# Two blocks of the expert product U moved beside the query projections, in buffers of their own

## The chip, the cores and the metric

The kernel runs on one core of a Trainium2 chip. The metric is the device time of one execution in microseconds (us), and lower is better. Engine names follow the profile: PE is TensorE (PEld its weight loads), DVE VectorE, ACT ScalarE, POOL GpSimd, SP SyncE; SPq and POOLq are their DMA queues.

## What is computed

The program is one decoder layer on 512 tokens of width 1024 in float32. Sparse attention, forgetting attention and their output projection come first. The part that matters here is the second half, PEER retrieval over 128 x 128 = 16384 single-neuron experts, with 8 heads of 16 experts each:

```python
q = (hc @ w_q).reshape(-1, PEER_HEADS, PEER_KEY_DIM)
s1 = einsum('chd,nd->chn', q[..., :half], k1); s2 = einsum('chd,nd->chn', q[..., half:], k2)
v1, i1 = top_k(s1, 16); v2, i2 = top_k(s2, 16)
best_s, best_pos = top_k(v1[..., :, None] + v2[..., None, :], 16)   # over the 256 sums
g = softmax(best_s)
act = gelu(einsum('cd,chkd->chk', hc, u[expert]))
out = einsum('chk,chkd->cd', g * act, v[expert])
```

## The kernel before, in words

**How PEER is computed.** The tokens stand in four tiles of 128. For tiles 0 to 2 nothing is gathered: U is multiplied with all 384 tokens, 128 blocks of 128 experts (`u_block`), each result goes through Gelu to a tile `a`, a dense matrix of gate weights (`gates`, p_g, stored in the DRAM tiles `g_d`) says how much each token wants of each expert, and V is multiplied with gates times `a` (`v_load`, `v_mm`, output acc). For tile 3 the chosen rows of U and V are gathered by indirect DMA (gu, gv) beside the V stage.

**Products in three parts.** `mm3` (L149 to L151) multiplies in three passes: each operand is split into a rounded part hi and a rest lo. So a block of U loads `raw` on SP's queue (L879), writes hi on ScalarE (L882), lo on VectorE (L887) or, for the odd blocks from 5 to 51, by ScalarE and an accumulating DMA on POOL's queue (L884, L885), and then has 8 x 3 = 24 matmuls of 384 columns (p_u). Gelu of the result is L893. The first 22 blocks store their `a` in DRAM (`a_d`, L895), since only 34 fit on the chip; the V stage reads those back as `ar` (L1004). The second operand is `h2`, the normed tokens of tiles 0 to 2; tile 3 has its own `h2l`.

**The stages around the change.** `residual` and `peer_norm` finish tile 3 (xn at L642, transposes at L647, hf at L650, h2l at L651 and L652). Then two halves of the query projection follow (p_q, `wchunks` of `w_pq` on L135 to L143), their transposes (tp_q, L863), and per tile and half a `route`: scores p_sc (L722, a bank of tag "tp") and sixteen best per side on VectorE (MAX8, MATCH_REPLACE8 and FIND_INDEX8, L729 to L733). Behind the projections their pool `wo` (in the stack `wst`) is closed and the pool `up` is opened on its memory (L869 to L871). `u_ahead(n)` (L901) makes the next n blocks, up to NAHEAD = 56: 4, then 2, then 2 in each of the 24 rounds of gates, then what is left. After that PSUM is handed over and the V stage begins, in which the other 72 blocks of U run between the blocks of V.

**What sets the order.** The framework orders the instructions of each engine when the program is built, by priority (the place in the program) and its own estimate of when each is ready; engines then run in that order. The load and the splits of a block carry a priority 1000 instructions ahead of their place (`tc.high_priority(offset=UPRI)`, L877); its matmuls have the priority of their place. Pools are stacked on two sides of SBUF; a tile in memory that a closed pool held waits, tile by tile, for the last user of what it overlaps. In `up` the blocks have three raw, two hi and three lo buffers and two for a stored `a`. Their PSUM banks go round the tags "pj", "po" and "ix", one bank each: "pj" also holds tp_q, "po" the attention's output, "ix" the transposes of `peer_norm`.

Of the kernel before, what the change touches and what calls it, by code (L numbers as in the profile page):

```python
# [9 lines left out]
F32 = mybir.dt.float32  # L10
F32R = mybir.dt.float32r
# [10 lines left out]
P = 128  # L22
D = 1024
KC = D // P
# [14 lines left out]
DT = ND * P  # L39
NACT = 34  # L40
# [15 lines left out]
PACE = 1.02  # L56
UPOOL = ()
LAST = 4
URB = 3
UDMA = tuple(range(5, 53, 2))  # L60
VRB = 3
# [15 lines left out]
def hybrid_layer(ctx: ExitStack, tc, x, pos, wada, wada_n, cols, w_small, w_in_a, w_in_b, wuk, wuv,  # L77
# [3 lines left out]
    def opened(stack, name, **kw):  # L81
        if "space" not in kw:
            kw["reuse_waits"] = "tile"
        return stack.enter_context(tc.tile_pool(name=name, bufs=1, **kw))
# [8 lines left out]
    def one(name, tag="tp"):  # L93
        return ps.tile([P, 512], F32, tag=tag, name=name, bufs=BANKS[tag])
# [53 lines left out]
    def mm3(o, ahi, alo, bhi, blo, start, stop, **kw):  # L148
        nc.tensor.matmul(o, ahi, bhi, start=start, stop=False, **kw)  # L149
        nc.tensor.matmul(o, ahi, blo, start=False, stop=False, **kw)  # L150
        nc.tensor.matmul(o, alo, bhi, start=False, stop=stop, **kw)  # L151
# [24 lines left out]
    def row_back(s, pl, tag, bufs):  # L176
        t = pl.tile([P, D], F32, tag=tag, name=f"gate{s}", bufs=bufs)
        nc.sync.dma_start(t, row_d[s].to_broadcast([P, D]))
        return t
# [95 lines left out]
    for half in range(2):  # L275
# [3 lines left out]
        for k in range(KC):  # L279
            a, b = eff[0][:, k:k + 1], mods[0][:, k:k + 1]  # L280
# [337 lines left out]
    wst = ExitStack()  # L618
# [86 lines left out]
    rt = ExitStack()  # L705
# [147 lines left out]
    for n in range(2):  # L853
# [12 lines left out]
                route(n, j - RLAG, *lists[j - RLAG])  # L866
        for j in range(NT - RLAG if n == 0 else NT, NT):
            route(n, j, *lists[j])
    wst.close()  # L869
    rq = opened(rt, "rq")  # L870
    up = opened(ctx, "up", side="right")  # L871


    acts = []

    def u_block(b, psum):
        with tc.high_priority(offset=UPRI):  # L877
            raw = up.tile([P, KC, P], F32, tag="raw", name=f"u{b}", bufs=URB)
            nc.sync.dma_start(raw.rearrange("p k e -> p (k e)"), ut[b])  # L879
            hi = up.tile([P, KC, P], F32R, tag="hi", name=f"uhi{b}", bufs=2)  # L880
            lo = up.tile([P, KC, P], F32R, tag="lo", name=f"ulo{b}", bufs=3)
            nc.scalar.activation(hi, raw, AF.Copy)  # L882
            if b in UDMA:
                nc.scalar.activation(lo, raw, AF.Copy, scale=-1.0)  # L884
                nc.gpsimd.dma_start(lo.rearrange("p k e -> p (k e)"), raw.rearrange("p k e -> p (k e)"), accum_op=ALU.add)  # L885
            else:
                (nc.gpsimd if b in UPOOL else nc.vector).tensor_tensor(lo, raw, hi.bitcast(F32), op=ALU.subtract)  # L887
        o = psum(f"p_u{b}")[:, :DT]
        for k in range(KC):
            mm3(o, hi[:, k], lo[:, k], h2[0][:, k], h2[1][:, k], k == 0, k == KC - 1)  # L890
        spilt = b < NSPILL
        a = up.tile([P, DT], F32, tag="as" if spilt else "a", name=f"a{b}", bufs=2 if spilt else NACT)
        nc.scalar.activation(a, o, AF.Gelu)  # L893
        if spilt:
            nc.sync.dma_start(a_d[b], a)  # L895
            a = a_d[b]
        acts.append(a)

    nu = [0]

    def u_ahead(n):  # L901
        for _ in range(n):
            if nu[0] < NAHEAD:
                u_block(nu[0], lambda n: one(n, ("pj", "po", "ix")[nu[0] % 3]))
                nu[0] += 1

    def chosen(j):
        sel3 = choose(j, *lists[j])
        if j == NT - 1:
            nc.vector.scalar_tensor_tensor(e0, sel3[:, 0], float(NK), sel3[:, 1], op0=ALU.mult, op1=ALU.add)  # L910
            nc.vector.tensor_copy(g0, sel3[:, 2])
        return sel3
# [30 lines left out]

    route(1, 0, *lists[0])
    u_ahead(U0[0])
    sel3 = chosen(0)
    u_ahead(U0[1])
    waiting = []

# [4 lines left out]
    for j, coming in ((0, (3, 1)), (1, (2,)), (2, ())):  # L954
        tt = spread(j, sel3)
        for tg in range(P // 16):
            for half in range(2):
                waiting.append((j, tg, half, hot(j, tg, half, *tt)))
            gates_all()
            for i, jn in enumerate(coming):  # L960
                if tg == WHEN[i][0]:
                    route(1, jn, *lists[jn])
                if tg == WHEN[i][1]:
                    sel3 = chosen(jn)
            u_ahead(GPAT[tg])
            for _ in range(NGP[tg] if j == ND - 1 else 0):
                next(gen)
# [14 lines left out]
    def v_load(b):  # L982
        if b % 8 == 0:
            gt = vp.tile([P, ND, P // 16, 8, 16], F32, tag="gt", name=f"gt{b}", bufs=2)
            for j in range(ND):
                nc.sync.dma_start(gt[:, j].rearrange("p g i t -> p g (i t)"),
                                  g_d[j][:, :, b:b + 8, :].rearrange("p g i t -> p g (i t)"))
            gts[0] = gt
        raw = vp.tile([P, D], F32, tag="raw", name=f"v{b}", bufs=VRB)
        nc.sync.dma_start(raw, pv[b * P:(b + 1) * P, :])  # L990
        late = b >= NK - LAST + VB
        if late:
            hi = up.tile([P, D], F32R, tag="hi", name=f"vhi{b}", bufs=2)
            lo = up.tile([P, D], F32R, tag="lo", name=f"vlo{b}", bufs=3)
        else:
            hi = vp.tile([P, D], F32R, tag="vhi", name=f"vhi{b}", bufs=VB)
            lo = vp.tile([P, D], F32R, tag="vlo", name=f"vlo{b}", bufs=VB)
        nc.scalar.activation(hi, raw, AF.Copy)  # L998
        nc.vector.tensor_tensor(lo, raw, hi.bitcast(F32), op=ALU.subtract)  # L999
        w = vp.tile([P, DT], F32, tag="w", name=f"w{b}", bufs=2)  # L1000
        a = acts[b]
        if b < NSPILL:
            a = vp.tile([P, DT], F32, tag="ar", name=f"ar{b}", bufs=ARB)
            nc.sync.dma_start(a, acts[b])  # L1004
        nc.vector.tensor_tensor(w.rearrange("p (g t) -> p g t", t=16), a.rearrange("p (g t) -> p g t", t=16),
                                gts[0][:, :, :, b % 8, :].rearrange("p j g t -> p (j g) t"), op=ALU.mult)
        if late:
            wh, wl = (up.tile([P, DT], F32R, tag="a", name=f"{n_}{b}", bufs=NACT) for n_ in ("wh", "wl"))
        else:
            wh = vp.tile([P, DT], F32R, tag="wh", name=f"wh{b}", bufs=VB)  # L1010
            wl = vp.tile([P, DT], F32R, tag="wl", name=f"wl{b}", bufs=VB)
        nc.scalar.activation(wh, w, AF.Copy)  # L1012
        last[0] = nc.vector.tensor_tensor(wl, w, wh.bitcast(F32), op=ALU.subtract).ins  # L1013
        return wh, wl, hi, lo
# [29 lines left out]

    steps = [RATE[0 if b < NSPILL else 1 if b < NK - NACT else 2] for b in range(NK - LAST)]
    due = 0.0
    tail = []
    for b in range(NK):
        ops = v_load(b)
        if b < NK - LAST:  # L1050
            for j in range(ND):
                v_mm(b, j, *ops)
        else:
            tail.append((b, ops))
        if b >= NSPILL and nu[0] < NK:
            u_block(nu[0], two)
            nu[0] += 1
        if b == NK - 24:
            gf = up.tile([P, D], F32, tag="raw", name="gf", bufs=URB)
            nc.sync.dma_start(gf, gfin.to_broadcast([P, D]))  # L1060
            gate2 = row_back(5, up, "raw", URB)
        if b < len(steps):
            due += steps[b] * (2 * TOPK - sum(NGP)) * PACE / sum(steps)
            while due >= 1.0:
                next(gen, None)
                due -= 1.0
# [69 lines left out]
```

## Time and profile before

| what | us |
|---|---|
| median of three runs | 1609.1 |
| lowest and highest run | 1595.54 and 1612.48 |
| the profiled execution | 1605.42 |
| its span in the trace | 1603.6 |

The span runs from the first to the last instruction of the trace. Times in the rows below are us from its start. A timeline row gives start, duration, engine, line, operation, output and inputs, the count, and in brackets the idle time ahead of it with what ended it.

### The profile page before, as it was taken

The numbers are of one execution on the slowest core, as the hardware profiler recorded it, in microseconds if no ns is written. First come the engines' busy times: TensorE is split into PE (matmuls) and PEld (weight loads), VectorE is DVE, ScalarE is ACT, GpSimd is POOL, SyncE is SP. The second block draws the span as 40 slices with busy tenths as digits, with TensorE's granted clock in tenths as the row PEclk, the third lists the DMA queues.
The fourth block names the chain that finished last, engine by engine and source line by source line (L and its number), as shares of the span: only waits on it lengthen the run. The fifth ranks groups of instructions, "written<-read, shape, count | busy, mean of one in ns | idle before, by whom it ended". The sixth has DMA issues, their size and how long they took to land.

```text
span 1603.6 us, 23086 instructions
## 1 busy us (share of the span) xinstructions
PE 1504.2 (94%) x8136; PEld 1321.3 (82%) x8138; DVE 1257.6 (78%) x2649; ACT 732.1 (46%) x1166; POOL 518.4 (32%) x413
## 2 busy tenths in 40 slices
PE   6888798998899999899999999999999999999996
PEld 6657587776699889789788999999999999998885
DVE  6698986856999999743567898888887888786886
ACT  4655446454156678665333333333333333333333
POOL 2323113112000220200013565554555555553420
PEclk7999899999999999999999999999999999999998
DMA  8233233522168987978877999999998999997974
GB/s 341 80 118 106 98 135 109 162 75 83 50 175 240 274 267 241 307 223 255 304 261 262 345 392 355 326 353 321 345 350 322 353 323 347 345 315 252 336 246 149
DMA packets 158277, 398.35 MB, mean 248 GB/s; under 512 B 12480, under 2 KB 68688, under 8 KB 154832
## 3 DMA queue, kind: packets, MB, share of 16 engines
q1 hardware_dynamic: 116832, 248.81, 46.2%
q0 software_dynamic: 40320, 146.82, 26.1%
q8 instruction: 64, 1.05, 0.3%
q10 hardware_dynamic: 1008, 1.24, 0.2%
q14 instruction: 53, 0.43, 0.1%
HBM read 350.54 MB, written 33.69 MB: 240 GB/s over the span
## 4 chain that ended last, share of the span: by engine, by line
PE 67%; DVE 12%; DMA 8%; ACT 6%; issue 5%; POOL 1%; SPq 0%; DVEq 0%; POOLq 0%; ACTq 0%
PE acc L1020 28%; PE p_u L151 9%; PE p_u L150 9%; PE p_u L149 9%; DMA ulo<-u 3%; PE po L562 2%; PE p_g L843 2%; ACT st L846 1%; PE p_b L149 1%; PE tp L552 1%; PE p_b L151 1%; PE p_b L150 1%; PE pl L536 1%; DMA wa<-in_wada_dram 1%; DVE ulo L887 1%
## 5 line engine op out<-in xcount | busy, mean ns | idle before, releaser
L151 PE MATMUL p_u<-h,ulo 128*128 128x384 f32 x1024 | 349.6, 341 | 10.2 <-DMA ulo<-u 10.1
L149 PE MATMUL p_u<-h,uhi 128*128 128x384 f32 x1024 | 348.9, 341 | 1.3 <-ACT a L893 1.3
L150 PE MATMUL p_u<-h,uhi 128*128 128x384 f32 x1024 | 347.1, 339 | 0.0
L919 POOL DMA_INDIRECT gu<-in_un_dram,e x128 | 191.3, 1495 | 275.4 <-DVE gu L927 238.6
L882 ACT ACTIVATE uhi<-u 128x1024 fp32r<-128x1024 f32 x128 | 135.9, 1062 | 283.5 <-PE p_u L150 277.7
L919 POOL DMA_INDIRECT gv<-in_pv_dram,e x128 | 195.5, 1527 | 180.4 <-DVE acc L938 153.2
L1020 PE MATMUL acc<-vhi,wh 128*128 128x512 f32 x768 | 237.3, 390 | 2.6 <-ACT wh L1012 2.6
L1020 PE MATMUL acc<-vlo,wh 128*128 128x512 f32 x768 | 237.4, 389 | 0.8 <-DVE vlo L999 0.8
L1020 PE MATMUL acc<-vhi,wl 128*128 128x512 f32 x768 | 237.0, 389 | 0.0
L1012 ACT ACTIVATE wh<-w 128x384 fp32r<-128x384 f32 x128 | 67.3, 526 | 316.3 <-issue 187.9
L151 PEld LDWEIGHTS p_u<-h,ulo 128*128 128x128 f32 x1024 | 194.5, 190 | 13.7 <-DMA ulo<-u 13.1
L149 PEld LDWEIGHTS p_u<-h,uhi 128*128 128x128 f32 x1024 | 194.6, 190 | 4.7 <-ACT a L893 1.7
L150 PEld LDWEIGHTS p_u<-h,uhi 128*128 128x128 f32 x1024 | 194.4, 190 | 3.6 <-issue 0.7
L1013 DVE TENSOR_TENSOR wl<-w,wh 128x384 fp32r<-128x384 f32 x128 | 71.3, 557 | 135.3 <-ACT wh L1012 135.1
L1020 PEld LDWEIGHTS acc<-vlo,wh 128*128 128x128 f32 x768 | 144.0, 188 | 31.3 <-DVE vlo L999 1.4
L1020 PEld LDWEIGHTS acc<-vhi,wl 128*128 128x128 f32 x768 | 144.2, 188 | 30.0
L938 DVE SCALAR_TENSOR_TENSOR acc<-gv,w,acc 128x1024 f32<-128x1024 f32 x127 | 162.4, 1279 | 5.6 <-DMA gv<-in_pv_dram,e 5.4
L1020 PEld LDWEIGHTS acc<-vhi,wh 128*128 128x128 f32 x768 | 143.2, 188 | 27.7 <-ACT wh L1012 3.3
L927 DVE SCALAR_TENSOR_TENSOR gu<-gu,h2n 128x1024 f32<-128x1024 f32 x128 | 154.0, 1220 | 15.4 <-DMA gu<-in_un_dram,e 15.4
L887 DVE TENSOR_TENSOR ulo<-u,uhi 128x1024 fp32r<-128x1024 f32 x104 | 126.9, 1220 | 49.3 <-ACT uhi L882 49.2
L999 DVE TENSOR_TENSOR vlo<-v,vhi 128x1024 fp32r<-128x1024 f32 x128 | 156.1, 1219 | 4.1 <-ACT vhi L998 3.8
L998 ACT ACTIVATE vhi<-v 128x1024 fp32r<-128x1024 f32 x128 | 135.5, 1059 | 10.2 <-PE acc L1020 4.3
(355 smaller groups left out, 2348.3 us busy)
## 6 DMA issues: line engine op xcount, KB each, us to landing
u<-in_ut_dram SPq DMA_DIRECT2D x128, 512.0 KB, 5.8
v<-in_pv_dram SPq DMA_DIRECT2D x128, 512.0 KB, 5.2
g_d<-st SPq DMA_DIRECT2D x24, 1024.0 KB, 6.2
gt<-g_d SPq DMA_DIRECT2D x48, 512.0 KB, 9.5
wada<-in_wada_dram SPq DMA_DIRECT2D x32, 512.0 KB, 3.3
ulo<-u POOLq DMA_DIRECT2D x24, 512.0 KB, 8.2
raw_b<-in_w_in_b_dram SPq DMA_DIRECT2D x12, 512.0 KB, 3.7
a_d<-a SPq DMA_DIRECT2D x22, 192.0 KB, 4.1
```

Of the source, the lines that this page charges most:

```text
L149: nc.tensor.matmul(o, ahi, bhi, start=start, stop=False, **kw)
L150: nc.tensor.matmul(o, ahi, blo, start=False, stop=False, **kw)
L151: nc.tensor.matmul(o, alo, bhi, start=False, stop=stop, **kw)
L882: nc.scalar.activation(hi, raw, AF.Copy)
L887: (nc.gpsimd if b in UPOOL else nc.vector).tensor_tensor(lo, raw, hi.bitcast(F32), op=ALU.subtract)
L919: nc.gpsimd.indirect_dma_start(out=t, out_offset=None, in_=src, in_offset=bass.IndirectOffsetOnAxis(ap=e0[:, s:s + 1], axis=0))
L927: nc.vector.scalar_tensor_tensor(t, t, 1.0, h2n, op0=ALU.mult, op1=ALU.mult, accum_out=dot0[:, s:s + 1])
L938: nc.vector.scalar_tensor_tensor(acc0, t, w0[:, s:s + 1], acc0, op0=ALU.mult, op1=ALU.add)
L998: nc.scalar.activation(hi, raw, AF.Copy)
L999: nc.vector.tensor_tensor(lo, raw, hi.bitcast(F32), op=ALU.subtract)
L1013: last[0] = nc.vector.tensor_tensor(wl, w, wh.bitcast(F32), op=ALU.subtract).ins
L1020: nc.tensor.matmul(accs[2 * j + n], l[:, js], r[:, n * 512:(n + 1) * 512], start=b == 0 and i == 0, stop=b == NK - 1 and i == 2)
```

## The change

Blocks 0 and 1 of U (`UEARLY = 2`) are issued at the end of the query projections, before the pool of the query weights is closed, from a pool `ue` of their own, opened under the same stack. It has one raw buffer, two hi, two lo and one stored `a`. The later blocks use `up` as before. The three PSUM tags are turned by one place, so that block 0 takes "po", block 1 "ix" and block 2 "pj". The calls of `u_ahead` behind it are as before.

```diff
+UEARLY = 2
...
-    wst.close()
-    rq = opened(rt, "rq")
-    up = opened(ctx, "up", side="right")
...
     def u_block(b, psum):
         with tc.high_priority(offset=UPRI):
-            raw = up.tile([P, KC, P], F32, tag="raw", name=f"u{b}", bufs=URB)
+            raw = up.tile([P, KC, P], F32, tag="raw", name=f"u{b}", bufs=URB if b >= UEARLY else 1)
             nc.sync.dma_start(raw.rearrange("p k e -> p (k e)"), ut[b])
             hi = up.tile([P, KC, P], F32R, tag="hi", name=f"uhi{b}", bufs=2)
-            lo = up.tile([P, KC, P], F32R, tag="lo", name=f"ulo{b}", bufs=3)
+            lo = up.tile([P, KC, P], F32R, tag="lo", name=f"ulo{b}", bufs=3 if b >= UEARLY else 2)
...
-        a = up.tile([P, DT], F32, tag="as" if spilt else "a", name=f"a{b}", bufs=2 if spilt else NACT)
+        a = up.tile([P, DT], F32, tag="as" if spilt else "a", name=f"a{b}", bufs=(2 if b >= UEARLY else 1) if spilt else NACT)
...
     def u_ahead(n):
         for _ in range(n):
             if nu[0] < NAHEAD:
-                u_block(nu[0], lambda n: one(n, ("pj", "po", "ix")[nu[0] % 3]))
+                u_block(nu[0], lambda n: one(n, ("po", "ix", "pj")[nu[0] % 3]))
                 nu[0] += 1
+
+
+    up = opened(wst, "ue", side="right")
+    u_ahead(UEARLY)
+    wst.close()
+    rq = opened(rt, "rq")
+    up = opened(ctx, "up", side="right")
```

## Rows read from the trace of the kernel before

**Rows 1.** The page: busy us, share of the span and instructions of each engine.
```profile
PE 1504.2 (94%) x8136; PEld 1321.3 (82%) x8138; DVE 1257.6 (78%) x2649; ACT 732.1 (46%) x1166; POOL 518.4 (32%) x413
```
**Rows 2.** The page: the chain that ended last, by engine and line.
```profile
PE acc L1020 28%; PE p_u L151 9%; PE p_u L150 9%; PE p_u L149 9%; DMA ulo<-u 3%; PE po L562 2%; PE p_g L843 2%; ACT st L846 1%; PE p_b L149 1%; PE tp L552 1%; PE p_b L151 1%; PE p_b L150 1%; PE pl L536 1%; DMA wa<-in_wada_dram 1%; DVE ulo L887 1%
```
**Rows 3.** Busy time by stretch; the last columns: granted clock, DMA share, GB/s.
```profile
375.30:379.00 3.70, 0.45 (x3) 0.21 (x2) 2.42 (x4) 1.90 (x4) 2.21 (x7) 0.97 0.88 302
...
428.20:435.20 7.00, 2.20 (x8) 1.60 (x8) 7.00 (x53) 3.19 (x4) 0.00 (x0) 0.87 0.43 150
435.20:440.20 5.00, 5.00 (x16) 4.55 (x15) 5.00 (x22) 0.00 (x0) 0.00 (x0) 0.50 0.44 136
...
430.00:768.00 338.00, 308.67 (x2175) 291.40 (x2175) 263.94 (x886) 222.86 (x271) 42.16 (x47) 0.97 0.81 248
```
**Rows 4.** Timeline of PE at the query projections.
```profile
359.74 0.60 PE L583 MATMUL tp_m<-cst_t,ob 128*128 128x128 f32 x4
...
378.79 1.12 PE L647 MATMUL tp_g<-cst_t,xn 128*128 128x128 f32 x4 [3.25 <-DVE xn L642]
...
429.07 0.66 PE L863 MATMUL tp_q<-cst_t,qn 128*128 128x128 f32 x4 [0.75 <-ACT qn L860]
433.77 2.08 PE L722 MATMUL p_sc<-keys_t,qT 128*128 128x256 f32 x4 [4.05 <-DVE iu L732]
```
**Rows 5.** Instructions on the raw tiles of U: duration ns min/median/max, first and last start.
```profile
L882 ACT ACTIVATE uhi<-u x128: 1042/1062/1121, 430.3 to 1435.8; 128x1024 fp32r<-128x1024 f32 x128
L887 DVE TENSOR_TENSOR ulo<-u,uhi x104: 1199/1220/1228, 435.1 to 1436.9; 128x1024 fp32r<-128x1024 f32 x104
...
DMA to landing us min/median/max: 3.4/6.4/14.9
```
**Rows 6.** Timeline of SP's queue at the first loads of U.
```profile
379.40 65.34 SPq L879 DMA_DIRECT2D u<-in_ut_dram  x6
```
**Rows 7.** Timeline of ACT at the first Gelu.
```profile
443.14 1.28 ACT L893 ACT_TABLE_LOAD   x1
444.44 0.49 ACT L893 ACTIVATE a<-p_u 128x384 f32<-128x384 f32 x1
```
**Rows 8.** Timeline of DVE from the last norm to the first routing.
```profile
384.76 0.70 DVE L651 CAST h2l<-hf 128x1024 fp32r<-128x1024 f32 x1 [5.42 <-ACT hf L650]
...
389.06 0.48 DVE L729 MAX8 v<-p_sc 128x8 f32<-128x128 f32 x2
```
**Rows 9.** Timeline of PE from the last gates to the first V block.
```profile
744.66 0.62 PE L843 MATMUL p_g<-oh,oh 128*128 128x128 f16 x8 [0.57 <-ACT st L846]
...
750.03 0.33 PE L149 MATMUL p_u<-h,uhi 128*128 128x384 f32 x1
...
754.19 0.33 PE L149 MATMUL p_u<-h,uhi 128*128 128x384 f32 x1
...
768.23 0.73 PE L1020 MATMUL acc<-vhi,wh 128*128 128x512 f32 x2 [1.68 <-ACT wh L1012]
```
**Rows 10.** Timeline of SP's queue from the last store of gates on.
```profile
747.27 0.33 SPq L849 DMA_DIRECT2D g_d<-st  x1
751.36 0.33 SPq L879 DMA_DIRECT2D u<-in_ut_dram  x1
...
755.52 0.34 SPq L879 DMA_DIRECT2D u<-in_ut_dram  x1
755.96 0.52 SPq L986 DMA_DIRECT2D gt<-g_d  x1
...
760.06 0.43 SPq L1004 DMA_DIRECT2D ar<-a_d  x1
```
**Rows 11.** DMA issues from 720 to 800: KB each, median us to landing.
```profile
gt<-g_d SPq DMA_DIRECT2D x9, 512.0 KB, 7.2
g_d<-st SPq DMA_DIRECT2D x3, 1024.0 KB, 6.2
```
**Rows 12.** Timeline of ACT ahead of the first V block.
```profile
767.65 0.52 ACT L1012 ACTIVATE wh<-w 128x384 fp32r<-128x384 f32 x1 [1.76 <-DVE w L1005]
```

## Prediction, made before the changed kernel was run

> **What bounds the kernel now.** The profiled execution took 1605.4 us for a span of 1603.6, so 1.8 us lie outside the span. The median of the three runs is 1609.1 (1595.5 to 1612.5). I sum against 1605.4 and add the 3.7 us between the two at the end. The page's busy line comes first: TensorE is at 94%, VectorE at 78% and the others below half [rows 1]. The chain that ended last agrees: most of it is TensorE, in p_u and in acc [rows 2]. So work taken off TensorE counts only if TensorE is busy where it is taken away, and work put on it is free only where TensorE is idle.
>
> The stage table shows such idle places at the query projections. In 375.3 to 379 TensorE is busy 0.45 us of 3.7; in 428.2 to 435.2 it is busy 2.2 of 7.0; and in 435.2 to 440.2, where block 0 of U starts, the granted clock is 0.50, the 1.2 GHz level, after that idle time [rows 3]. The instructions name the causes. The first hole is 3.25 us before the transposes of the last tile's norm, waiting for VectorE's xn. The second is 4.05 us before p_sc, waiting for VectorE's index search (L732): the top-16 routing has filled VectorE by then [rows 4]. From 430 to 768 TensorE is busy 308.7 us of 338 [rows 3], so there it is the limit, with some 9% of stalls.
>
> **Part 1: two blocks leave the late stage.** A block is 24 matmuls. Two of them that are 24 matmuls apart start at 750.03 and 754.19, so a block takes 4.16 us, 0.173 us a matmul [rows 9], and two take 8.3. The number of blocks made ahead stays 56, and the calls behind the change ask for 4, 2, 24 times 2, and then for what is left. Before, 2 are left for the very end; now none are. So two blocks go from behind the last gates to before the first: -8.3 us of TensorE work after 768 at the most.
>
> **Part 2: the same two run earlier.** The new pool lies just below the query weights, on memory of the attention stage. Its raw tile falls on the last attention outputs, which the transposes of L583 read at 359.74 [rows 4]; the hi and lo tiles fall on older ones. So u0 can be loaded from about 360.4. From block times in the trace (load to landing 6.4 us, hi 1.06, lo 1.22 [rows 5]) block 0 is split by about 369, and block 1, which shares the single raw buffer, by about 379. h2 of the three tiles they multiply is long there. Block 0 can use bank "po" at once. Block 1 needs "ix", which the last norm gives back near 384. Their matmuls were issued behind the projections in the program, so they fill holes: 3.25 us at 375.5, and 4.05 us at 429.7 with 0.75 us of waiting ahead of it. That is 8.05 us of cover for 8.3 us of work: +0.3. If they are put between projections instead, the projections end later, but p_sc then waits so much less for VectorE, and the sum is the same. Without any cover the cost would be 8.3.
>
> The other instructions of the moved steps: two loads of 512 KB and two stores of 192 KB on SP. SP issued six loads of u from 379.40 over 65 us [rows 6], so it was waiting for memory and not for its turn; the moved ones stand ahead of these and delay nothing, unless u0 is queued before 360 and holds up the projection weights (a rival below). On ScalarE hi and Gelu, 1.06 and 0.49 us per block [rows 5, 7], find an engine that is busy 1.9 of 3.7 and 3.2 of 7.0 us in the two holes [rows 3]. On VectorE two lo of 1.22 us fit in the 5.42 us of idle time before h2l [rows 8]; if they fall behind 389, where VectorE is full, they cost 2.4. That is also what VectorE saves later; I count nothing for it (bounds 0 and -2.4), because from 430 on TensorE is the fuller of the two, 308.7 us against 263.9 [rows 3].
>
> **Part 3: the clock.** In 435.2 to 440.2 there are 16 matmuls in 5.0 us, which take 16 x 0.173 = 2.8 at 2.4 GHz. If blocks 0 or 1 run in the hole before, block 2 starts at full clock: -2.2 us. The bounds are 0, when the hole stays, and -2.2.
>
> **Part 4: what waits next at the other end.** The gain of part 1 has to pass the start of the V stage. The last p_g starts at 744.66 and is done at 745.28; the first acc starts at 768.23, 22.95 us behind it. In between lie nearly five blocks of p_u, to 766.5, and then 1.68 us of idle time [rows 9]. After the change nearly three blocks are left, 12.5 us. But the V stage also needs the gates: the store g_d is issued at 747.27 [rows 10], 2.0 us behind the last p_g, lands 6.2 us later, and gt, read back from it, needs 7.2 us [rows 11]; then wh, 0.52 [rows 12], behind w, which is a product of the same size and taken as long. That makes 2.0 + 6.2 + 7.2 + 1.1 = 16.5 us, if nothing else holds SP. SP's queue shows that something does: prefetches of u are issued at 751.36 and 755.52, each when a raw buffer comes free, and only behind them gt's third part at 755.96 and ar at 760.06 [rows 10]. These loads (u56 to u58 before, u58 to u60 after) are paced by the blocks behind the last gates, so they can stand in the same place: 22.95 us, no gain at all. Bounds 16.5 and 22.95, and I take the middle, 19.7, since neither end is nearer to a row: -3.2 us instead of -8.3.
>
> TensorE is then idle from 12.5 to 19.7 us, longer than the 4.05 us that left it at 0.50 before. The V stage starts cold: +2.2 by the same 5 us stretch (bounds 0, for V loads that are late anyway, and 2.5).
>
> The moment of the last p_g itself moves little: 52 blocks stand ahead of the last gates in the program before (0 to 51), and behind 435 just as many after (2 to 53). It gains part 3's 2.2 and loses part 2's 0.3.
>
> **Sum.** -2.2 + 0.3 - 3.2 + 2.2 = -2.9. 1605.4 - 2.9 = 1602.5 in the profiled run's terms, 1606.2 as a median.
>
> A rule of the Trainium skill that speaks against the change: Gelu of block 0 moves the first table load to about 380, ahead of the last norm's hf. The row shows 1.28 us, with Gelu 0.02 us behind it [rows 7]. The Trainium skill ("ScalarE: Activation LUTs", What ACT_TABLE_LOAD costs) states 1283 ns and a drain of about 1380 ns, 2.66 us for each switch. By the row the last norm can be 1.3 us later, by the page 2.7; the sum would go to -1.6 or -0.2. The trace shows no such drain here, so I stay with the row, and with nothing, as VectorE's chain has its idle time there.
>
> **Rivals.**
> *The V stage follows TensorE* (all of the gain arrives). The prefetches of u fall behind gt and ar in SP's queue, or the gates are read back earlier. Then -8.3 - 2.2 + 0.3 = -10.2: 1598.9 as a median. For it: five blocks, not the store, ended last before. Against: 16.5 us of store and load behind the last p_g are more than 12.5 us of blocks; fully it needs the last gates to come earlier too.
> *Nothing moves* (the change does not do what it says). The two blocks are queued on TensorE behind the last projection, or their splits are; the hole is then filled by work that leads to the same last gates, and SP's queue keeps the 22.95 us. 0, or 1609.
> *Slower.* The splits carry a priority 1000 instructions ahead of their place, so ScalarE and VectorE can take them in front of the last norm, whose result starts VectorE's routing at 389.06 [rows 8]; from there VectorE is full until the first gates. Price: two hi, two lo, a table load and two Gelu, 2.1 + 2.4 + 1.3 + 1.0 = 6.8 us on that chain, with the tail of 22.95 unchanged and the clock not regained: +6.8, 1616. It decides as soon as the first MAX8 of the routing comes more than some 3 us later than now. For it: SP, ScalarE and VectorE work in order, so one early wait holds all behind it. Against: VectorE had 5.42 us free just there.
> *Another order.* The build orders each engine's instructions anew; shifts of some us elsewhere (splits by DMA that come late, an eviction before a gate) can have either sign, 5 us or so.
>
> **How the numbers follow.** Forecast 0.45, full gain 0.22, nothing 0.13, slower 0.12, another order 0.08. A 1% change, 16 us, is about what a measurement can tell from none here. The largest gain that can be worked out is 10.2 us, the largest loss 6.8, and the runs of the same kernel spread by 17; so a result outside 1% needs a rival and a lucky run together: faster 0.10, slower 0.05, same 0.85. The range holds the rivals' ends, 1599 and 1616, and part of that spread: 1592 to 1618.
>
> **What would show it.** Right: p_u in the stretch 375 to 435 and the hole before p_sc gone; a clock near 1 in 435 to 440; the last p_g within 3 us of now, less than three and a half blocks behind it, and a new idle time of TensorE of 4 to 10 us before the first acc, put down to V loads, gt or ar. Wrong: no p_u before 430; the first MAX8 later than 392; a first acc more than 8 us earlier than 768, or later; or a change in the V stage behind 840, where each block takes the same work in both.

## The result: 23 us slower, where no change was forecast

| | before | after |
|---|---|---|
| median, us | 1609.98 | 1632.57 |
| lowest and highest run | 1595.54 and 1612.48 (4 runs) | 1626.93 and 1633.84 (4 runs) |
| the profiled execution, its span | 1605.42, 1603.6 | 1632.45, 1630.7 |

The ratio is 1.0162, with a 95% interval of 1.0125 to 1.02 (the two medians alone give 1.0140). The forecast was 1606.2 (1592 to 1618), with 0.05 for slower. The runs of most kernels here, the one before included, lie in two groups some 10 us apart, so a median of four moves by some us with the share of each; the experiments below have up to 25 runs of before beside them, at a median of 1600.3 to 1607.6.

**Where the time went.** The last acc matmul ends at 1591.6 before and at 1618.2 after, 26.6 us later. Four marks on TensorE's timeline cut this up: the start of the first p_sc, the end of the last p_g, the start of the first acc and the end of the last acc.

| stretch, us | before | after | difference |
|---|---|---|---|
| start to first p_sc | 386.3 | 393.0 | +6.7 |
| first p_sc to last p_g | 358.9 | 376.9 | +18.0 |
| last p_g to first acc | 23.0 | 22.1 | -0.9 |
| first to last acc | 823.4 | 826.2 | +2.8 |

The first row is not the change's (see the run of before below). The second is: 52.1 blocks of U (p_u matmuls over 24) stand in it before, 54.1 after. TensorE is busy 330.4 us of it before and 337.9 after, and idle for 28.6 and 39.1. So 7.5 us of work, a little less than two blocks at 4.16 us [rows 9], and 10.5 us of stalls make the 18.0.

The waits of TensorE after, from 340 to 500 us (total, times, longest):

```profile
PE p_q L151 <- DVE wlo_pq L144: 8.8, 1, 8.8
PE p_u L152 <- DVE ulo L884: 3.6, 1, 3.6
PE tp_g L648 <- DVE xn L643: 3.6, 2, 2.0
PE p_u L152 <- DMA ulo<-u: 2.7, 1, 2.7
PE p_sc L723 <- DVE iu L733: 0.9, 2, 0.5
```

The change does what it says: the 4.05 us hole before p_sc [rows 4] is gone; all waits of p_sc are 0.9 us. But a new wait stands on top, twice as long, and it is for something that the change never touched: wlo_pq, the rest lo of a chunk of the query weights. The busy time by stretch shows it (as in [rows 3]: the stretch and its length; busy time of PE, PEld, DVE, ACT and POOL with the counts; granted clock, DMA share, GB/s):

```profile
422.60:433.70 11.10, 10.52 (x57) 9.58 (x55) 11.10 (x79) 0.49 (x1) 0.74 (x2) 1.00 0.05 18
433.70:442.40 8.70, 0.00 (x0) 0.00 (x0) 8.70 (x65) 0.49 (x1) 0.00 (x0) 0.63 0.24 83
442.40:455.70 13.30, 12.51 (x54) 9.63 (x54) 9.55 (x72) 5.73 (x9) 0.69 (x2) 0.86 0.14 45
```

In the first stretch TensorE runs the two early blocks, at the full clock. In the second it does nothing, VectorE is full, and the granted clock falls to 0.63. The hole that was to be filled has come back behind its filling. VectorE's timeline after, from the first early lo on, tells who took whose place:

```profile
387.04 1.23 DVE L884 TENSOR_TENSOR ulo<-u,uhi 128x1024 fp32r<-128x1024 f32 x1 [0.92 <-ACT uhi L879]
391.41 0.69 DVE L652 CAST h2l<-hf 128x1024 fp32r<-128x1024 f32 x1 [3.15 <-ACT hf L651]
392.14 1.23 DVE L653 TENSOR_TENSOR h2l<-hf,h2l 128x1024 fp32r<-128x1024 f32 x1
394.35 1.23 DVE L884 TENSOR_TENSOR ulo<-u,uhi 128x1024 fp32r<-128x1024 f32 x1 [0.99 <-ACT uhi L879]
395.50 0.49 DVE L730 MAX8 v<-p_sc 128x8 f32<-128x128 f32 x2
...
441.70 0.67 DVE L144 TENSOR_TENSOR wlo_pq<-raw_pq,whi_pq 128x512 fp32r<-128x512 f32 x1
```

And the same place on VectorE before, between h2l's second part and the first MAX8 of [rows 8]:

```profile
387.79 1.35 DVE L143 TENSOR_TENSOR wlo_pq<-raw_pq,whi_pq 128x512 fp32r<-128x512 f32 x1 [1.07 <-ACT whi_pq L141]
```

Before, the last split of the query weights (chunk 7 of the second half) has the last slot ahead of the routing. After, the lo of block 1 has it, by its priority lift. The loop over the two halves issues the splits of the second half behind the routing of the first, so in the program this one stands behind that routing; with the slot gone the build puts the routing ahead of it. Counted from the first p_sc, it runs 48.7 us behind in place of 1.5, so 47 us later. All four p_q of the second half need it. TensorE's timeline after, at the end of the hole:

```profile
433.30 0.34 PE L152 MATMUL p_u<-h,ulo 128*128 128x384 f32 x1
442.43 0.80 PE L151 MATMUL p_q<-wlo_pq,h 128*128 128x512 f32 x1 [8.79 <-DVE wlo_pq L144]
```

Behind it the next blocks are late too, since the pool `up` waits for the query weights' memory: ScalarE's first uhi from `up` starts at 454.61 (430.3 before [rows 5]), which is the 3.6 us wait for ulo in the list.

**The other end** went in the main as the prediction's part 4 says. SP's queue after, from the last store of gates on:

```profile
771.91 0.33 SPq L850 DMA_DIRECT2D g_d<-st  x1
775.99 0.33 SPq L876 DMA_DIRECT2D u<-in_ut_dram  x1
776.42 1.31 SPq L990 DMA_DIRECT2D gt<-g_d  x2
780.14 0.34 SPq L876 DMA_DIRECT2D u<-in_ut_dram  x1
780.58 0.52 SPq L990 DMA_DIRECT2D gt<-g_d  x1
```

And TensorE's last p_g and first acc after:

```profile
769.29 0.62 PE L844 MATMUL p_g<-oh,oh 128*128 128x128 f16 x8 [0.52 <-ACT st L847]
...
792.01 1.22 PE L1024 MATMUL acc<-vhi,wh 128*128 128x512 f32 x2 [4.12 <-ACT wh L1016]
```

As before [rows 10] each load of u, paced by a block, stands ahead of a part of gt. There are 3.9 blocks in this stretch (4.7 before), and the idle time ahead of the first acc is 4.12 us (1.68 before [rows 9]): 22.1 us in place of 22.95. The two blocks that were to leave the end gave back 0.9 us, and they stand in front of the gates with 7.5 us of work.

The idle time has a price behind it too. The first 8 us of the V stage, before and after:

```profile
768.20:776.20 8.00, 7.97 (x35) 6.63 (x36) 5.44 (x8) 2.92 (x4) 0.00 (x0) 1.00 0.68 253
```

```profile
792.00:800.00 8.00, 7.99 (x24) 6.35 (x25) 3.53 (x5) 2.48 (x3) 0.00 (x0) 0.64 0.81 280
```

At a granted clock of 0.64 TensorE gets 24 matmuls into the time of 35. By these counts that costs some 2.5 us (an estimate), about the 2.8 in the last row of the table above.

### The profile page after: what moved, and what is told of

Its sections match the earlier page's. It is cut to its first block, busy times and chain, and to the rows that moved or that the text cites. A ratio compares the mean times of both kernels' runs of the same rounds, so it can differ in the third digit from the quotient of the medians.

```text
span 1630.7 us, 23085 instructions
## 1 busy us (share of the span) xinstructions
PE 1515.9 (93%) x8136; PEld 1332.1 (82%) x8138; DVE 1256.2 (77%) x2649; ACT 733.7 (45%) x1166; POOL 520.9 (32%) x413
## 4 chain that ended last, share of the span: by engine, by line
PE 64%; DVE 12%; issue 5%; DMA 4%; ACT 4%; POOL 1%; SPq 0%; DVEq 0%; POOLq 0%; ACTq 0%
PE acc L1024 28%; PE p_u L152 9%; PE p_u L150 8%; PE p_u L151 8%; DMA ulo<-u 2%; PE po L563 2%; DVE oh L828 1%; PE p_g L844 1%; DVE ulo L884 1%; PE pl L537 1%; PE p_b L150 1%; PE tp L553 1%; ACT st L847 1%; PE p_b L151 1%; PE p_b L152 1%
## 5 line engine op out<-in xcount | busy, mean ns | idle before, releaser
L1002 ACT ACTIVATE vhi<-v 128x1024 fp32r<-128x1024 f32 x128 | 135.6, 1059 | 23.2 <-issue 8.7
```

## The experiments

Theory A: the loss is the starved split. Theory B: it is the blocks themselves, whose time ahead of the last gates is not given back behind them. Theory C: the front. `U0` holds the first two numbers that `u_ahead` is called with, (4, 2) before and after. Beside the ratio to before, the table has times in us from the first p_sc of each profile, which leaves the front out, and the blocks of U between it and the last p_g.

| kernel | ratio (95%) | p_q waits for the split | blocks | last p_g | first acc |
|---|---|---|---|---|---|
| before | | no | 52.1 | 358.9 | 381.9 |
| before again | one run | no | 52.1 | 353.9 | 377.1 |
| after | 1.0162 (1.0125 to 1.02) | 8.8 | 54.1 | 376.9 | 399.0 |
| before, split late | 1.0134 (1.0072 to 1.0197) | 12.9 | 52.1 | 381.6 | 403.0 |
| after, U0 = (2, 2) | 1.0134 (1.0098 to 1.017) | 8.8 | 52.1 | 369.4 | 391.1 |
| after, split on GpSimd | 1.0077 (1.0042 to 1.0113) | no | 54.1 | 363.2 | 384.5 |
| after, split lifted | 1.0083 (1.0051 to 1.0115) | no | 54.1 | 362.6 | 384.1 |
| after, early blocks not lifted | 1.0078 (1.0037 to 1.012) | no | 54.1 | 364.5 | 386.5 |
| before, U0 = (6, 2) | 1.0085 (1.005 to 1.012) | no | 54.1 | 373.2 | 394.3 |
| after, split on GpSimd, U0 = (2, 2) | 0.997 (0.9936 to 1.0005) | no | 52.1 | 351.3 | 373.5 |
| after, split lifted, U0 = (2, 2) | 0.9985 (0.9953 to 1.0018) | no | 52.1 | 351.3 | 373.1 |
| after, one early block, U0 = (3, 2) | 1.0014 (0.9986 to 1.0042) | no | 52.1 | 359.3 | 380.8 |
| after, split lifted, U0 = (2, 0) | 1.0046 (1.0018 to 1.0073) | no | 50.1 | 353.0 | 380.8 |
| before, split on GpSimd | 1.0039 (1.001 to 1.0068) | no | 52.1 | 361.7 | 383.5 |

The two profiles of before differ by 5 us in the last columns, so they carry no difference smaller than that; the ratios do.

### The split on another engine

```diff
-                eng = nc.vector if k % 4 in DVE_LO.get(name.rstrip("0123456789"), ()) else nc.gpsimd
+                eng = nc.vector if k % 4 in DVE_LO.get(name.rstrip("0123456789"), ()) and (name, k) != ("pq1", 7) else nc.gpsimd
```

> The changed kernel with one split moved: the lo part of the last chunk (k=7) of the second half of the query weights goes to GpSimd instead of VectorE. Theory A (starved split: the two early lo of U take the one slot that this split had on VectorE ahead of the routing, it then waits behind three routings, and TensorE waits 8.8 us for it at 433.6 to 442.4 while the memory of the weights comes free late): the hole in front of p_q is gone, block 2 of U starts about 13 us earlier, and the time falls from 1632.6 by 15 to 25 us, to 1608 to 1618. Rival B (the two blocks themselves, their clock and the new order of the late stage cost the 22 us): the time stays within 6 us of 1632. Rival C (the queries' 7 us that the trace of the changed kernel was already late at 300 us belong to the change): 1620 to 1626.

1612.5 us, 20 less than the changed kernel. The wait of p_q is gone; the waits of TensorE from 340 to 500 us are:

```profile
PE p_u L152 <- DMA ulo<-u: 3.8, 3, 2.0
PE tp_g L648 <- DVE xn L643: 3.6, 2, 2.0
PE p_sc L723 <- DVE iu L733: 1.5, 3, 0.7
```

So at least half of the loss is A's (by the ratios 0.85% of the 1.62%), and 0.8% is left.

### The split late, with no block moved

In the kernel before, the same split waits for the last VectorE instruction of the routing of tile 2.

```diff
+    routed = {}
...
+                with tc.issue_after(routed[0, 2]) if (name, k) == ("pq1", 7) else nullcontext():
-                eng.tensor_tensor(lo[:, :n], raw[:, kk, :n], hi[:, :n].bitcast(F32), op=ALU.subtract)
+                    eng.tensor_tensor(lo[:, :n], raw[:, kk, :n], hi[:, :n].bitcast(F32), op=ALU.subtract)
...
-            nc.vector.max_index(bp[:, 8:16], bv[:, 8:16], wk_)
+            routed[n, j] = nc.vector.max_index(bp[:, 8:16], bv[:, 8:16], wk_).ins
```

> The kernel before, with one edit: the same split (lo of chunk k=7 of the second half of the query weights, on VectorE) is ordered behind the last VectorE instruction of the routing of tile 2. No block of U is moved. Theory A: TensorE stands still for 15 to 20 us in front of p_q (here no early block fills any of it), block 2's counterpart, block 0, starts some 12 us later than 435, and the time rises to 1622 to 1632. Rival B: the order of this one split costs less than 5 us, 1608 to 1615.

1628.4 us, 1.0134: most of the loss, without the change. The wait was to be 15 to 20 us and is 12.9. The wait, and a stretch of it in which nothing fills it:

```profile
PE p_q L153 <- DVE wlo_pq L146: 12.9, 1, 12.9
```

```profile
433.80:443.80 10.00, 0.00 (x0) 0.00 (x0) 10.00 (x74) 0.00 (x0) 0.00 (x0) 0.50 0.00 0
```

### The early blocks without their lift

```diff
-        with tc.high_priority(offset=UPRI):
+        with tc.high_priority(offset=UPRI) if b >= UEARLY else nullcontext():
```

> The changed kernel without the priority lift for the loads and splits of blocks 0 and 1 (the later blocks keep it). In the order built, both lo of U then come behind the routing and the split of the weights keeps its place ahead of it. Theory A: no hole in front of p_q, 1605 to 1615, near the kernel before, as the blocks are no longer early. Rival B (pools, banks or the shorter tail cost the time): 1622 or more.

1614.7 us. The early lo now come behind the routing, from 435.02 on, and the split has its old slot (387.60). With the starvation the change's gain is gone too: p_sc waits 4.1 us at once again. What stays is the same 0.8% as with the split on GpSimd, though the early blocks do nothing early here. That speaks for B: what both have in common is 54 blocks ahead of the last gates.

### Two blocks less ahead of the gates

The split on GpSimd by the diff above, and:

```diff
-U0 = (4, 2)
+U0 = (2, 2)
```

> The split on GpSimd as above, and U0 = (2, 2) instead of (4, 2), so that the two early blocks are taken out of the first group and two blocks are left for the end, as in the kernel before. If the last gates move with the number of blocks issued ahead of them, they come 8 us earlier than with U0 = (4, 2), five blocks lie behind them again, and the time is 3 to 8 us below the run with the split on GpSimd alone. Rival (the V stage starts with the end of the blocks in both): within 2 us of it.

1598.7 us, 0.997: with both faults undone the kernel is level with before, and the last p_g is 12 us earlier than with the split alone moved. That is 13.8 us less than the run with the split alone, where 3 to 8 were expected: two blocks cost more than the time of their matmuls.

### The control: the split on GpSimd in the kernel before

```diff
-                eng = nc.vector if k % 4 in DVE_LO.get(name.rstrip("0123456789"), ()) else nc.gpsimd
+                eng = nc.vector if k % 4 in DVE_LO.get(name.rstrip("0123456789"), ()) and (name, k) != ("pq1", 7) else nc.gpsimd
```

> The kernel before, with the last weight split (chunk 7 of the second half, lo) on GpSimd and nothing else. It is the control for the two runs that moved this split in the changed kernel. Theory A (the change's loss is this split's place behind the routing): here the split is not late, so its engine makes no difference; ratio 0.997 to 1.003, last gates 357 to 361 us behind the first p_sc (358.9 before), 52 blocks of U in between. Rival (the split on GpSimd is a gain or a loss of its own, by which the earlier runs are misread): a ratio off by 0.5% or more, with the same sign in the two earlier runs.

1.0039 (1.001 to 1.0068): a miss. Moved alone, this split costs a little. It does not explain the two runs above, which were faster than the changed kernel, but it leaves their remainder open by some 0.4%, so the remedy was also tried without a change of engine (below). Against this control, the run with both faults undone (0.997) is some 0.7% faster, and the two intervals do not meet.

### The blocks alone, in the kernel before

```diff
-U0 = (4, 2)
+U0 = (6, 2)
```

> The kernel before, with U0 = (6, 2) in place of (4, 2): 54 blocks of U between the first p_sc and the last gates in place of 52, none kept for the end, no early buffers. Theory B (two blocks put ahead of the last gates cost their time there, and the V stage, which waits for those gates, gives none of it back): last gates 8.3 us later (367 us behind the first p_sc), last gates to first acc 22 us as before, 6 to 10 us in all, ratio 1.004 to 1.007. Rival (the 0.8% of the two versions with the split in time comes from the early blocks themselves, their buffers, banks or order): ratio 0.998 to 1.002, with the tail shorter by what the gates are later.

1.0085, a little over what was expected. Two blocks more ahead of the gates cost 12.7 us by the medians (1612.98 against 1600.29), though nothing is early and the split is in time. That is more than the 8.3 us of their matmuls. In this profile the waits for the lo that come by DMA are longer too. TensorE from 490 to 775 us:

```profile
PE p_u L151 <- DMA ulo<-u: 15.7, 5, 7.0
PE p_g L843 <- ACT st L846: 6.4, 12, 0.6
```

The wait for ulo is 9.1 and 5.3 us between first and last p_g in the two profiles of before. Whether two more blocks always lengthen it is not shown: with the split on GpSimd it is 10.7 us with 52 blocks (the control) and 10.1 with 54. Behind the gates little comes back: last p_g to first acc takes 21 us with 3.9 blocks in it, against 23 in the two profiles of before.

### The split late, two blocks less

The changed kernel, with no other edit:

```diff
-U0 = (4, 2)
+U0 = (2, 2)
```

> The changed kernel, with U0 = (2, 2): two blocks less ahead of the last gates, two kept for the end; the split still late. Theories A and B as two separate sums: the wait of p_q for the split of 8 to 9 us stays, the two blocks (8.3 us and some stalls, 12 us between the two versions with the split on GpSimd) leave, so 1632.6 - 8 to 12 = 1620 to 1625, ratio to before 1.010 to 1.014. If the loss is all the split's (B false): as the changed kernel, 1.015 to 1.018. If it is all the blocks': 1.000 to 1.004.

1622.6 us, 1.0134, as the two sums have it. The two blocks alone, with the split late in both, are worth 7.9 us at the first acc, and 0.3% by ratios whose intervals overlap.

### The split kept on VectorE, with a lift of its own

```diff
+                with tc.high_priority(offset=UPRI) if (name, k) == ("pq1", 7) else nullcontext():
-                eng.tensor_tensor(lo[:, :n], raw[:, kk, :n], hi[:, :n].bitcast(F32), op=ALU.subtract)
+                    eng.tensor_tensor(lo[:, :n], raw[:, kk, :n], hi[:, :n].bitcast(F32), op=ALU.subtract)
```

> The changed kernel, with the same priority lift for the last weight split as the blocks of U have; it stays on VectorE, behind the two early lo and ahead of the first MAX8 of the routing. Theory A, in the form that the order of priorities did it: as with the split on GpSimd, no wait of p_q for it above 2 us, ratio 1.005 to 1.011 (1.0077 with the split on GpSimd). Rival (VectorE's work did it: three splits of 1.2, 1.2 and 0.7 us in front of the routing delay it whatever their order): the ratio stays at 1.012 or more, and the first gates come over 103 us behind the first p_sc.

1.0083, as on GpSimd. VectorE now does all three splits around the first MAX8:

```profile
387.49 1.23 DVE L885 TENSOR_TENSOR ulo<-u,uhi 128x1024 fp32r<-128x1024 f32 x1 [0.99 <-ACT uhi L880]
388.63 0.49 DVE L731 MAX8 v<-p_sc 128x8 f32<-128x128 f32 x2
389.04 1.38 DVE L145 TENSOR_TENSOR wlo_pq<-raw_pq,whi_pq 128x512 fp32r<-128x512 f32 x1
```

The 1.38 us in front of the routing cost nothing that can be seen; the first gates come 100.4 us behind the first p_sc (101.6 before, 104.5 after). So the order did it, not VectorE's work.

### The kernel before once more

No edit.

> The kernel before once more, for a second profile of it. Theory C (the 7 us by which the changed kernel was already late at the first p_sc belong to the change) has the first p_sc at 386 us again, within 1 us; its rival (the front differs from run to run with the granted clock, since the order is the same on every engine up to there) lets it stand anywhere from 385 to 398, with a lower granted clock between 150 and 290 us where it is late. From the first p_sc on both expect what the first profile shows: first gates 101 to 103 us, last gates 357 to 361, last acc 1201 to 1206.

The first p_sc came at 386.4, as before. That alone would fit C. But the run with `U0 = (6, 2)`, whose program is that of before up to here, had it at 395.1, and the one with `U0 = (2, 2)` and the lift at 398.3, where the one with the lift alone had 386.2. So the front moves by up to 12 us between runs, and C falls. The other expectation missed as well: the last p_g came 353.9 us behind the first p_sc, where 357 to 361 were expected, with no edit at all. That is the 5 us by which two profiles of one kernel differ. Where the front is late the stretch from 250 to 300 us shows a lower granted clock; before, after, and before with `U0 = (6, 2)`:

```profile
250.00:300.00 50.00, 44.05 (x267) 35.92 (x266) 37.16 (x69) 32.77 (x91) 15.56 (x14) 0.97 0.52 165
```

```profile
250.00:300.00 50.00, 42.42 (x233) 35.09 (x234) 32.78 (x58) 29.38 (x79) 15.48 (x13) 0.90 0.38 126
```

```profile
250.00:300.00 50.00, 42.60 (x224) 36.53 (x223) 28.70 (x53) 28.30 (x76) 15.50 (x13) 0.83 0.36 110
```

### Both undone, the split on VectorE

The lift of the split as above, and:

```diff
-U0 = (4, 2)
+U0 = (2, 2)
```

> The changed kernel with both faults undone: the last weight split has the priority lift (it stays on VectorE), and U0 = (2, 2), so 52 blocks of U stand ahead of the last gates as in the kernel before, two of them run in the holes of the projections, and 4.7 blocks cover the wait for the gates. Theories A and B: what is left is the change's own gain, the holes (3 to 5 us of stalls less between the first p_sc and the first gates) and the clock behind them; last gates 348 to 355 us behind the first p_sc (358.9 before), first acc 22 us later, ratio 0.991 to 0.998. Against them: a ratio of 1.000 or more says that a third cost of the change is left.

0.9985 (0.9953 to 1.0018): the interval ends on both sides of 1, and the ratio is just above the 0.991 to 0.998 that were expected. In the profile the change's own gain is there: the two blocks fill the hole, and the stretch around it (the front of this run is 12 us late, so it holds the place of 428 to 440 before) is full and at the full clock,

```profile
430.00:455.00 25.00, 23.85 (x124) 21.00 (x124) 25.00 (x166) 6.56 (x9) 1.40 (x4) 1.00 0.33 101
```

and the first acc comes 4 to 9 us earlier than in the two profiles of before, counted from the first p_sc. The medians don't show it. With the split on GpSimd in both, the same comparison gives 0.7% (0.997 against 1.0039). So whether the change by itself is worth some us or none stays open.

### Two more blocks kept for the end

The lift of the split as above, and:

```diff
-U0 = (4, 2)
+U0 = (2, 0)
```

> As the run with U0 = (2, 2) and the lift, with U0 = (2, 0): 50 blocks ahead of the last gates, six behind. Theory B, whole: the wait from the last gates to the first acc has a floor of some 21 to 22 us that the gates' way through memory sets, and a length that TensorE sets once the blocks behind the last gates are longer than that. Here 5.9 blocks stand there, 24.5 us and 1.4 for the handover of the banks, so the last gates come 8 us earlier than in that run and the first acc only 3 to 5 us earlier, ratio 0.989 to 0.997. Rival (the blocks ahead of the gates cost more than their time, so that fewer are better without end): first acc 8 to 12 us earlier, ratio 0.985 to 0.990.

1.0046: the tail grew to 27.8 us, as expected, but the last p_g did not move (353.0 against 351.3). Both theories miss the reason. A store of gates stood in SP's queue behind loads of u that waited for a buffer, and the evictions of p_g waited for that store, so that p_g then waited 9.7 us for ScalarE. The longest such wait of p_g was 2.1 us with U0 = (2, 2). SP's queue and then ScalarE, in this run:

```profile
655.85 16.18 SPq L877 DMA_DIRECT2D u<-in_ut_dram  x3
672.08 0.90 SPq L851 DMA_DIRECT2D g_d<-st  x2
```

```profile
678.62 3.70 ACT L848 ACTIVATE st<-p_g 128x512 f32<-128x512 f32 x4 [9.70 <-DMA g_d<-st]
```

So fewer blocks ahead of the gates do not help without end, and the rival falls; that a block costs its time there is shown from 52 to 54 blocks only.

### One early block

```diff
-U0 = (4, 2)
+U0 = (3, 2)
...
-UEARLY = 2
+UEARLY = 1
```

> The changed kernel with one early block in place of two (UEARLY = 1) and U0 = (3, 2), so that 52 blocks stand ahead of the last gates and two are kept for the end, as in the kernel before; no other edit, no lift. Theory A: it was the second block's lo that took the last slot of VectorE ahead of the routing. With one block the split keeps its slot: no wait of p_q for it above 2 us, first gates 100 to 103 us behind the first p_sc, last gates 348 to 356, ratio 0.993 to 1.001. Rival (any early block of U holds the split up, or the early load does): a wait of p_q of 8 us or more, ratio 1.010 or more.

1.0014 (0.9986 to 1.0042), just above the range that was expected, with the last gates at 359.3 in place of 348 to 356. But the split has its slot, without a lift, and the rival's 1.010 is out. VectorE's timeline around it:

```profile
395.63 1.23 DVE L653 TENSOR_TENSOR h2l<-hf,h2l 128x1024 fp32r<-128x1024 f32 x1
397.94 1.34 DVE L144 TENSOR_TENSOR wlo_pq<-raw_pq,whi_pq 128x512 fp32r<-128x512 f32 x1 [1.08 <-ACT whi_pq L142]
399.20 0.48 DVE L730 MAX8 v<-p_sc 128x8 f32<-128x128 f32 x2
```

It was the second block's lo that starved it, not the first's.

## Why the prediction was wrong, point by point

**The step that failed** is in part 2: "On VectorE two lo of 1.22 us fit in the 5.42 us of idle time before h2l; if they fall behind 389, where VectorE is full, they cost 2.4." One lo did fit: h2l starts 1.6 us ahead of the first p_sc in both kernels. The other fell into the 2 us behind h2l, and its cost was not its length but its place. The step asked how long VectorE would be busy with what the change adds, and not which instruction stood in the slot that it took, and where that one goes: the split that ran at 387.79, between the two rows of [rows 8]. Its price by the runs is the difference between late and in time at equal blocks. With 52 blocks that is 1.0134 against 0.9985, 18.0 us at the first acc; with 54 it is 1.0162 against 1.0083, 14.9 us. In each pair the intervals don't meet.

**The second failure** is the sentence "The moment of the last p_g itself moves little", with the +0.3 of part 2. The count was right, two blocks more between the first p_sc and the last gates. The cover was not. It was to be 8.05 us of holes, 3.25 of them before the transposes of the last norm. That hole could not be used: u0 was taken to be loaded from 360.4 and split by 369. SP's queue after shows it behind the weights:

```profile
359.58 3.45 SPq L136 DMA_DIRECT2D raw_pq<-in_w_pq_dram  x2
...
373.18 6.64 SPq L136 DMA_DIRECT2D raw_pq<-in_w_pq_dram  x3
379.87 0.46 SPq L876 DMA_DIRECT2D u<-in_ut_dram  x1
...
388.29 0.33 SPq L876 DMA_DIRECT2D u<-in_ut_dram  x1
```

So the lo were done at 388.3 and 395.6 in place of 369 and 379 (6.7 us of that are the late front), just ahead of the routing, where the weight split stands. Of the 8.3 us some 4.8 (4.05 and 0.75) had cover. The price of two blocks more, by the runs: 1.0083 against 0.9985 with the split lifted, 1.0% or 11.0 us at the first acc; and 0.85% in the kernel before. The two faults together, from 373.1 to 399.0 at the first acc, are 25.9 us, against 18.0 and 11.0 for each alone: they add up within the 5 us that two profiles differ by. By the ratios they are 1.8% together, against 1.5% and 1.0% alone, so how exactly they add up is not shown.

**What bounds the kernel** was read rightly: TensorE from the projections on, with the holes named. **Part 1** took the 8.3 us to leave the stretch behind the last gates; of 4.7 blocks 3.9 stay there, as later blocks of U move up. **Part 3** was right in kind: where the hole goes the clock is 1.00 (the stretch of both faults undone) in place of 0.50 [rows 3]; in the changed kernel the new hole takes it down again, 0.63 and 0.86. **Part 4** was right in its mechanism, and the most useful: the V stage hangs on the gates' way through SP's queue. Between its two ends the value taken was 19.7 us; measured were 22.1, near the upper end of 22.95, and 21.0 to 23.2 in the other profiles with 3.9 or 4.7 blocks behind the gates. Its cold start of the V stage, +2.2, came as forecast, though after 4.12 us of idle time and not some 7: the clock is 0.64 in the first 8 us. With the idle time of 3.0 to 4.0 us in the other runs with 54 blocks it is 0.79 or 0.80 there, and 1.00 in every run with 52, where the idle time is at most 1.9 us.

**The sentence on the table load.** It came at 406.22 and took 1.28 us, not at about 380, and the next Gelu came 21 us behind it. It delayed nothing; the sum would not have moved by the Trainium skill's figure ("ScalarE: Activation LUTs", What ACT_TABLE_LOAD costs) either. No run shows the drain of 1380 ns that the Trainium skill adds there: Gelu stood 0.02 us behind the load before [rows 7].

**The rivals.** "The V stage follows TensorE" fell with part 4. "Slower" had the right engines, SP, ScalarE and VectorE in order, and the right side, but the wrong victim: it had the splits delay the first MAX8. That came at 395.50, later than the 392 it named, but with the front; behind the first p_sc it stands 2.5 us after and 2.7 us before. A mark in absolute time could not tell the two apart. And it capped the loss at 6.8 us, the length of what was added, so the range ended 14.6 us short of the result.

## What to carry to other kernels

When an instruction with a lift is put into a gap of an engine that is full right behind it, look for the instruction of low priority that lives in that gap, and who waits for it: its loss here was not a slot but the whole full stretch (47 us for 0.67 us of work). Work that moves from behind a dependency to ahead of it costs its time there, and gives it back behind only where that work, and not the dependency itself, set the time. So count the blocks ahead of the last gates, and not only the holes. And where the front of a kernel varies, measure a mark from the last event that the change can't have touched.

## What was not expected of the hardware

The program up to the first p_sc took between 385.4 and 398.3 us in the profiles. The two runs with the split on GpSimd in the changed kernel have the same instructions in the same order up to there, and took 385.4 and 397.6. From 250 to 300 us the granted clock was 0.97, 0.90 and 0.83 in the three rows above, with 44.05, 42.42 and 42.60 us of work on TensorE and a DMA rate of 165, 126 and 110 GB/s. What starts a run on the one side or the other was not tried.
